# Program order for a log-decay stage, and what stands in front of the modulation dots, in a gated-linear-attention layer on one core

## The chip, the core and the metric

The kernel runs on one core of a Trainium2 chip. The core has a TensorE (PE; its weight loads are shown as PEld), a VectorE (DVE), a ScalarE (ACT), a GpSimd (POOL) and a SyncE (SP), which here issues the DMAs. Each engine works through its own queue in order and waits on semaphores. Matmuls write to PSUM banks; everything else lies in SBUF or in the chip's DRAM. The metric is the device time of one execution in microseconds (us), lower being better.

## What is computed

One layer: a token mixer (bidirectional gated linear attention in four heads beside a short convolution) and a convolutional feed-forward, over 1024 tokens of width 1024, with 256 context tokens that only give the attention its first states. Cut to what matters here:

```python
sh1, sc1, gt1, sh2, sc2, gt2 = split(silu(c) @ w_ada + b_ada, 6)        # modulation of the tokens
csh1, csc1, ... = split(silu(c_ctx) @ w_ada + b_ada, 6)                  # and of the context
hc = rmsnorm(ctx, g_pre_mix) * (1 + csc1) + csh1
pc = hc @ w_in[:, :COL_Q]                    # context keys, values, low-rank gate inputs
k, v, g_f, g_b = gla_inputs(pc)              # g = log_sigmoid(a_low @ w + b) / 16, per head and channel
s_f, s_b = gla_final_state(...)              # sum of k * exp(b_last - b) times v, b = cumsum(g)
p = (rmsnorm(x, g_pre_mix) * (1 + sc1) + sh1) @ w_in
o = gla(q, k, v, g_f, s_f) + flip(gla(flip(...), s_b))
o_gla = rmsnorm(o, g_head) * silu(og)
o_sc = sb * (w_sc[0] * left + w_sc[1] * u + w_sc[2] * right + b_sc)      # u = sc * sx, in rows of 64
x = x + gt1 * rmsnorm(concat(o_gla, o_sc) @ w_out, g_post_mix)
x = x + gt2 * rmsnorm(conv_ffn(...), g_post_ffn)
```

Products are made with about float32 accuracy: each operand is split into a rounded part `hi` and a remainder `lo` (`split`, L130: ACT copies to `hi`, DVE or POOL subtracts), and `mm3` (L142) sums three products.

## The kernel before

The program is straight-line: every loop is unrolled. TensorE runs in program order throughout. For ACT, DVE, POOL and SP a planner orders the instructions from simulated times and priorities, except inside `tc.manual_schedule(engines=...)`, where the named engines keep program order. A tile takes a buffer of its pool when its first writer is planned; that writer waits on the chip for the buffer's last reader.

**Token-major pass** (L577 to L628; ACT, DVE and POOL in program order, SP planned). 128 tokens at a time, `token_major` (L516) makes 24 matmuls of 272 columns with the tokens as the stationary operand. The first round (`g` = 2, L588, tk 0 to 7) gives the low-rank gate inputs (`als`) and 240 value columns, then context keys (`kc`, L604) and context values (`vc`, L614); the second round (`g` = 1, L618) gives the remaining 272 value columns for tokens and context. The weights of the second round are loaded by `wa_load(1, kt)` and split by `wa_split(1, kt)`: kt 0 to 3 at the end of the first round, kt 4 to 7 after the context values (L616). `ctx_norm` (L492) transposes and modulates the context two feature tiles at a time and returns the subtraction that makes their lo part (`ctx_lo`, L510). `put_aT` (L528) transposes the gate inputs of one token tile and stores them three times (hi, lo, and the raw value, which is rounded on writing).

**Modulation dots.** `w_ada` is streamed in tiles of 512 KB, 48 of them in this pass (16 for the context, 32 for the later parts of the tokens); each is multiplied with the conditioning row and summed by one DVE instruction (`ada_dot`, L231). `some_ada(n)` (L547) first does the dots of the loads that the previous call issued, then issues `n` loads into buffers lent by other pools (`few` and `many`, L544: `px`, `wraw`, `whi`, `wlo`, `ada`).

**Weight blocks.** `block(n)` (L573) streams 128 columns of `w_in` in all eight row tiles: a DMA to `raw`, `hi` on ACT at once, and `rest()`, a generator of four POOL subtractions. Block 2 is made at the end of the pass (L622), the others by `stream` (L654): `halves` (L639) multiplies a block with 512 tokens at a time, in two steps of four row tiles (12 matmuls of 512 columns each); blocks come in threes, product, second factor, third factor, of the short convolution (`sc_first`, `sc_conv`, `sc_last`).

**Log-decay stage and recurrence.** `gla()` (L723) is a generator that yields how many steps of `stream` are due; the loop at L994 interleaves the two. Its first eleven steps are the log-decay stage: two context tiles (`ctx_decay`), eight token tiles (`decay`: one gate matmul, three ACT instructions, one DVE instruction, L476), context keys' weights (`ctx_keys`, L791), cumulative sums by a triangular matrix (`sums`, L737, copied by ACT to `bc`), the context state (`ctx_state`, L804) and the first keys' weights `kx` (`kx_prep`, L753: small exponentials to `dec`, difference, exponential, product). Gate matmuls take turns in two PSUM banks (`ps_at`), and `ctx_keys`, `sums` and `ctx_state` in two others (`ps_ms`). DVE keeps program order for the first two steps only (`ORDERED = 2`); ACT is planned. Then come `kx_turn` and `update` for eight tiles, the levels of the attention, and the output.

**Output projection** (from L1229). The first two token tiles' inputs are loaded and split under a written order of ACT, DVE and SP (L1233): `so` is the convolution half, `sog` the gates, `mix_first` splits `so`, `mix_gate` applies the SiLU gate.

Of the kernel before, what the change touches and what calls it, by code (L numbers as in the profile page):

```python
# [8 lines left out]
F32 = mybir.dt.float32  # L9
# [110 lines left out]
def build(nc, ap, out, dbg=None):  # L120
# [6 lines left out]
    def act(o, i, fn=AF.Copy, **kw):  # L127
        return S.activation(o, i, fn, **kw)  # L128
# [20 lines left out]
    with tile.TileContext(nc) as tc, tc.manual_schedule(engines={mybir.EngineType.PE}):  # L149
# [378 lines left out]
        def put_aT(tk):  # L528
            pt = bank(ps_ms)
            PE.transpose(pt[:32, :P], als[tk], ident)  # L530
            s = slice(tk * P, (tk + 1) * P)
            act(aT[0:32, s], pt[:32, :P])
            V.tensor_tensor(aT[32:64, s], pt[:32, :P], aT[0:32, s].bitcast(F32), ALU.subtract)
            V.tensor_copy(aT[64:96, s], pt[:32, :P])

        def xlhs(tk):
            s = slice(tk * P, (tk + 1) * P)
# [6 lines left out]
        few = (px, "x", 8), (wp, "wraw", 2), (pgt, "ada", 1), (px, "x", 8), (wp, "wraw", 2)  # L544
        many = (px, "x", 8), (wp, "whi", 2), (pgt, "ada", 1), (wp, "wlo", 2), (px, "x", 8), (wp, "whi", 2), (wp, "wlo", 2)

        def some_ada(n, where=few):  # L547

            for a, raw in pend:
                ada_dot(a[0], a[1], raw)  # L550
            pend.clear()
            for _ in range(n):
                a = next(adas, None)
                if a is not None:
                    where_ = where[nada[0] % len(where)]
                    pend.append((a, ada_load(a[0], *where_)))
                    nada[0] += 1

        def stream_weights(src, eng):
            raw = wp.tile([P, KT, P], F32, tag="wraw", name=nm("wr"))  # L560
            SY.dma_start(raw, src)
            hi = wp.tile([P, KT, P], F32R, tag="whi", name=nm("wh"))
            lo = wp.tile([P, KT, P], F32R, tag="wlo", name=nm("wl"))
            act(hi, raw)

            def rest():
                for k in range(0, KT, 2):
                    eng.tensor_tensor(lo[:, k : k + 2], raw[:, k : k + 2], hi[:, k : k + 2].bitcast(F32), ALU.subtract)  # L568
                    yield

            return hi, lo, rest()
# [5 lines left out]
        with tc.manual_schedule(engines={mybir.EngineType.Activation, mybir.EngineType.DVE, mybir.EngineType.Pool}):  # L577
            ctx_load()
            some_ada(4)
            for hf in range(2):  # L580
                pq1 = bank(ps_mm)
                tsl = slice(hf * 512, hf * 512 + 512)
                for kt in range(KT):
                    mm3(pq1, wq1[kt], (hxh[kt][:, tsl], hxl[kt][:, tsl]), kt == 0, kt == KT - 1)
                act(qh[hf][:, 1, :], pq1, AF.Copy, scale=DK ** -0.5)
            for t in range(NT):
                vt[t] = pvo.tile([P, VW], F32, tag="vo", name=nm("v"))
            for tk in range(NT):  # L588
                some_ada((3, 3, 3, 2, 2, 1, 2, 2)[tk])
                if 4 <= tk < 8:  # L590
                    ctx_lo()
                token_major(2, tk, xlhs(tk), vt[tk])
                if tk > 1:
                    put_aT(tk - 2)
                if 3 <= tk < 7:
                    ctx_lo = ctx_norm(tk - 3)
                if tk == NT - 1:
                    for kt in range(4):
                        wa_load(1, kt)
                        wa_split(1, kt)  # L600
            put_aT(NT - 2)
            kc = px.tile([P, NCT, QK], F32, tag="x", name="kc")
            vc = px.tile([P, NCT, VW], F32, tag="x", name="vc")
            for j in range(NCT):  # L604
                pp = bank(ps_mm)
                some_ada(3)
                for kt in range(KT):
                    mm3(pp[:, :QK], hc(kt, j), (wah[0, kt][:, :QK], wal[0, kt][:, :QK]), kt == 0, kt == KT - 1)
                act(kc[:, j, :], pp[:, :QK])
            put_aT(NT - 1)  # L610
            for kt in range(4, KT):
                wa_load(1, kt)
            some_ada(3)
            for j in range(NCT):  # L614
                token_major(2, NT + j, lambda kt: hc(kt, j), vc[:, j, :])
            for kt in range(4, KT):  # L616
                wa_split(1, kt)
            for tk in range(NT):  # L618
                some_ada((3, 3, 3, 3, 3, 2, 0, 0)[tk], many)
                token_major(1, tk, xlhs(tk), vt[tk])  # L620
                if tk == NT - 2:
                    w2 = block(2)  # L622
                    for _ in w2[2]:
                        pass
                if 0 < tk <= NCT:
                    put_aT(NT + tk - 1)
            for j in range(NCT):
                token_major(1, NT + j, lambda kt: hc(kt, j), vc[:, j, :])  # L628
# [10 lines left out]
        def halves(w, nxt, dests):  # L639

            hi, lo = w[:2]
            for hf in range(2):
                bk = bank(ps_mm)
                s = slice(hf * 512, hf * 512 + 512)
                for kt in range(KT):
                    mm3(bk, (hi[:, kt, :], lo[:, kt, :]), (hxh[kt][:, s], hxl[kt][:, s]), kt == 0, kt == KT - 1)
                    if kt == KT // 2 - 1:
                        next(nxt[2], None)
                        yield
                dests(hf, bk)  # L650
                next(nxt[2], None)
                yield

        def stream():  # L654
            w = w2
            for n in range(16):
# [8 lines left out]
                    yield from halves(w, nxt, lambda hf, bk: og_out(n - 12, hf, bk))  # L665
                w = nxt

        def sc_tile(dt=F32):
            return pg_.tile([P, 512], dt, tag="sc", bufs=4, name=nm("sc"))

# [4 lines left out]
        def sc_conv(j, hf, bk, us):  # L675
            u = us[hf]
            V.tensor_tensor(u, u, bk, ALU.mult)
            y = sc_tile()
            act(y, u, AF.Identity, bias=col("bsc", j), scale=col("wsc", 3 * j + 1))
            y3, u3 = (a.rearrange("p (r c) -> p r c", c=GW) for a in (y, u))  # L680
            V.scalar_tensor_tensor(y3[:, :, 1:], u3[:, :, :-1], col("wsc", 3 * j), y3[:, :, 1:], ALU.mult, ALU.add)
            V.scalar_tensor_tensor(y3[:, :, :-1], u3[:, :, 1:], col("wsc", 3 * j + 2), y3[:, :, :-1], ALU.mult, ALU.add)
            us[hf] = y

        def sc_last(j, hf, bk, us):
            y = us[hf]
# [28 lines left out]
            split(wo_raw(0), hi, lo)  # L715
            woh[worder[0]], wol[worder[0]] = hi, lo

        ORDERED = 2
        on = [None] * NT
        pe_ = popen("pe_", "right", bufs=1)  # L720
        flat = lambda t: t.rearrange("p f t -> p (f t)")
# [1 line left out]
        def gla():  # L723
# [26 lines left out]

            kxs, kxt = {}, {}

            def kx_prep(hf, d):  # L753
                e = (P - 1) if d == 0 else 0
                for hh in range(2):
                    act(decv[d * DK : d * DK + DK, hh, :, 4 * hf : 4 * hf + 4],
                        bc[hf][d][hh * DK : hh * DK + DK].rearrange("p f (c t) -> p f c t", t=P)[:, :, :, e],
                        AF.Exp, scale=ITAU)
                kx = pe_.tile([P, 2, 512], F32, tag="e", bufs=4, name=nm("kx"))
                b3 = bc[hf][d].rearrange("p f (c t) -> p (f c) t", t=P)  # L760
                V.tensor_tensor(kx.rearrange("p f (c t) -> p (f c) t", t=P),
                                b3[:, :, e : e + 1].broadcast_to([P, 8, P]), b3, ALU.subtract)
                act(kx, kx, AF.Exp, scale=ITAU)
                V.tensor_tensor(kx, kx, kh[hf], ALU.mult)
                kxs[hf, d] = kx

            def kx_turn(c):
                pt = bank(ps_at)
# [52 lines left out]
            for c in range(NT):  # L821
                decay(c)
                if c == 2:
                    V.tensor_copy(masks, mraw)
                if 0 < c <= NCT:
                    ctx_keys(c - 1)
                if c > 1:
                    sums(c - 2)
                if c == 4:
                    su = [px.tile([P, 2, 512], F32, tag="x", name=f"su{i}") for i in range(4)]  # L830
                    ctx_state()
                if c in (5, 6):
                    kx_prep(0, c - 5)
                yield 0.8 if c > 1 else 1
            sums(NT - 2)
            yield 0.8
# [1 line left out]
            for c in range(NT):  # L838
# [6 lines left out]
                if c > 0:  # L845
                    update(c - 1)
                if c in (1, 2):
                    kx_prep(1, c - 1)
                yield 1.2
            update(NT - 1)  # L850

# [134 lines left out]
                    yield 0.8  # L986

        ga, st = gla(), stream()
        with tc.manual_schedule(engines={mybir.EngineType.DVE}):
            for _ in range(ORDERED):  # L990
                next(st)
                next(ga)
        due = 0.0
        for steps in ga:  # L994
            due += steps
            while due >= 1:
# [236 lines left out]
        with tc.manual_schedule(engines={mybir.EngineType.Activation, mybir.EngineType.DVE, mybir.EngineType.SP}):  # L1233
            so = pvo.tile([P, H, P], F32, tag="vo", name=nm("so")), t7[:, 0, :].rearrange("p (h t) -> p h t", t=P)
            dma(so[0], sc_d[0][0])
            sog = [gate_load(c) for c in range(2)]
            dma(so[1], sc_d[0][1])
            wo_raw(6)
            xts = [x1_load(c) for c in range(2)]
            wo_split(1)  # L1240
# [1 line left out]
            wo_split(2)  # L1242
            wo_split(3)
            wo_raw(7)
            mix_gate(0, sog[0])
            made.append(mix_first(so[1]))
            wo_split(4)
            split(sog[0], *(t[:, 0:4, :] for t in made[0]))
            mix_gate(1, sog[1])
# [451 lines left out]
```

## Time and profile before

| | |
|---|---|
| median of 3 runs | 1142.1 us (1141.63 to 1143.94) |
| profiled execution | 1145.11 us, its span 1143.3 us |
| granted TensorE clock, mean | 0.996 |
| idle TensorE, 0 to 75 / 75 to 150 / 150 to 197 us | 8.2 / 2.1 / 5.7 us |
| idle TensorE, 197 to 400 / 400 to 1143 us | 1.6 / 9.5 us |
| HBM read / written | 142.12 / 32.78 MB |

The idle times are the length of each stretch less the TensorE's busy time in it. A timeline row of the profile gives start, duration, engine, line, operation, output<-inputs, and in brackets the idle time before it with the instruction that ended it. L128 and L135 are the lines of helpers (`act`, the subtraction of `split`), so such rows are told apart by their tiles. A granted clock of 0.50 means that the TensorE runs at half its speed.

### The profile page before, as it was taken

How to read it: one execution, taken by the hardware profiler on the slowest of the kernel's cores; microseconds unless marked ns; L12 is line 12 of the kernel's file. 1: busy time of each engine (PE TensorE's matmuls, PEld its weight loads, DVE VectorE, ACT ScalarE, POOL GpSimd, SP SyncE). 2: the span in 40 equal slices, each digit the busy share in tenths (PEclk: the TensorE clock that was granted, in tenths of full speed). 3: DMA queues.
4: the chain of work that ended last, by engine and by line, in shares of the span. 5: the costliest groups of instructions: out<-in, count | busy, mean ns of one | idle time of the engine just before them, and what ended most of it. 6: DMA issues, size and time to landing. Idle time of an engine off the chain costs nothing. (4 is left out here: it accounts for less than half of the span.)

```text
span 1143.3 us, 16858 instructions
## 1 busy us (share of the span) xinstructions
PE 1116.2 (98%) x6256; PEld 924.3 (81%) x6256; DVE 874.5 (76%) x1193; ACT 523.6 (46%) x941; POOL 490.1 (43%) x465
## 2 busy tenths in 40 slices
PE   8999989999999999999999999999999999999997
PEld 7689977888887878887888888888888888888885
DVE  5979845699777465677799887887878788777676
ACT  6744167654343366565323333324242445544443
POOL 5200031347466111128787787777778670000002
PEclk9999999999999999999999999999999999999999
DMA  9987962312113274231244223322323269978572
GB/s 354 303 284 243 348 108 58 95 43 67 53 32 102 62 245 145 83 125 66 86 148 142 98 83 111 124 98 74 120 99 106 79 228 353 333 241 287 189 240 101
DMA packets 80132, 176.00 MB, mean 154 GB/s; under 512 B 9807, under 2 KB 21711, under 8 KB 80050
## 3 DMA queue, kind: packets, MB, share of 16 engines
q1 hardware_dynamic: 80050, 174.93, 46.1%
q8 instruction: 49, 0.80, 0.3%
q14 instruction: 33, 0.27, 0.1%
HBM read 142.12 MB, written 32.78 MB: 153 GB/s over the span
## 5 line engine op out<-in xcount | busy, mean ns | idle before, releaser
L1373 DVE SCALAR_TENSOR_TENSOR y<-u,cols,y 128x945 f32<-128x945 f32 (+2 forms) x176 | 214.8, 1222 | 3.7 <-ACT y L128 1.3
L145 PE MATMUL ps<-mx,p 128*128 128x512 f32 x440 | 173.5, 394 | 0.9 <-DVE g L1428 0.5
L146 PE MATMUL ps<-mx,p 128*128 128x512 f32 x440 | 172.5, 392 | 0.0
L147 PE MATMUL ps<-mx,p 128*128 128x512 f32 x440 | 172.5, 392 | 0.0
L135 POOL TENSOR_TENSOR p<-rs,p 128x512 fp32r<-128x512 f32 x88 | 116.6, 1329 | 86.1 <-ACT p L128 86.1
L568 POOL TENSOR_TENSOR wl<-wr,wh 128x256 fp32r<-128x256 f32 x64 | 57.9, 935 | 163.6 <-ACT wh L128 163.5
L147 PE MATMUL ps<-p,p 128*128 128x512 f32 x308 | 120.0, 390 | 0.2
L146 PE MATMUL ps<-p,p 128*128 128x512 f32 x308 | 119.9, 389 | 0.0
L145 PE MATMUL ps<-p,p 128*128 128x512 f32 x308 | 119.9, 389 | 0.0
L145 PE MATMUL ps<-hxh,wh 128*128 128x512 f32 x256 | 104.0, 406 | 1.0 <-DVE sc L687 1.0
L147 PE MATMUL ps<-hxh,wl 128*128 128x512 f32 x256 | 100.8, 394 | 0.0
L145 PEld LDWEIGHTS ps<-mx,p 128*128 128x128 f32 x440 | 82.5, 188 | 22.5 <-ACT u L128 3.2
L146 PE MATMUL ps<-hxl,wh 128*128 128x512 f32 x256 | 100.6, 393 | 0.0
L128 ACT ACTIVATE p<-rs 128x512 fp32r<-128x512 f32 x88 | 54.5, 623 | 100.6 <-POOL rs L1198 100.6
L147 PEld LDWEIGHTS ps<-mx,p 128*128 128x128 f32 x440 | 82.6, 188 | 18.7
L146 PEld LDWEIGHTS ps<-mx,p 128*128 128x128 f32 x440 | 82.6, 188 | 18.2
L135 POOL TENSOR_TENSOR p<-wr,p 128x512 fp32r<-128x512 f32 x57 | 74.0, 1298 | 10.9 <-ACT p L128 10.9
L128 ACT ACTIVATE y<-u,cols 128x1024 f32<-128x1024 f32 x22 | 26.6, 1210 | 102.9 <-DVE u L1435 102.9
L147 PE MATMUL ps<-b,p 128*128 128x512 f32 x176 | 69.5, 395 | 0.0
L145 PE MATMUL ps<-b,p 128*128 128x512 f32 x176 | 69.4, 394 | 0.0
L146 PE MATMUL ps<-b,p 128*128 128x512 f32 x176 | 69.4, 394 | 0.0
L147 PEld LDWEIGHTS ps<-p,p 128*128 128x128 f32 x308 | 57.8, 188 | 12.9 <-DVE p L135 0.8
(278 smaller groups left out, 2611.8 us busy)
## 6 DMA issues: line engine op xcount, KB each, us to landing
ada<-in_ada SPq DMA_DIRECT2D x64, 512.0 KB, 5.3
wr<-in_wu SPq DMA_DIRECT2D x48, 512.0 KB, 4.0
h<-hd SPq DMA_DIRECT2D x77, 256.0 KB, 4.3
hd<-h SPq DMA_DIRECT2D x73, 256.0 KB, 2.0
wdr<-in_wd SPq DMA_DIRECT2D x55, 256.0 KB, 3.3
wdr<-in_wd SPq DMA_DIRECT2D x22, 512.0 KB, 6.0
x<-in_x SPq DMA_DIRECT2D x16, 512.0 KB, 4.5
wr<-in_wb SPq DMA_DIRECT2D x16, 512.0 KB, 3.7
```

Source lines behind the costliest of these rows:

```text
L128: return S.activation(o, i, fn, **kw)
L135: (eng or V).tensor_tensor(lo, raw, hi.bitcast(F32), ALU.subtract)
L145: PE.matmul(ps, lh, rh, start=first, stop=False, skip_group_check=more)
L146: PE.matmul(ps, lh, rl, start=False, stop=False, skip_group_check=more)
L147: PE.matmul(ps, ll, rh, start=False, stop=last, skip_group_check=more)
L568: eng.tensor_tensor(lo[:, k : k + 2], raw[:, k : k + 2], hi[:, k : k + 2].bitcast(F32), ALU.subtract)
L1373: V.scalar_tensor_tensor(y3[:, ro, co], u3[:, ri, ci], col("wcf", 9 * p + 3 * (dr_ + 1) + dc + 1), y3[:, ro, co], ALU.mult, ALU.add)
```

## The change

- In the first round, the context's lo part and `put_aT` (its transposes too) go in front of the dots. The third store of `put_aT` is done by ACT instead of DVE.
- `some_ada` is parted: `ada_loads` only issues loads. The keys' loop asks for two loads a time instead of three, and the call before the context values issues two loads and does no dots, so the splits of the value weights (L616) follow without dots between. The second round asks for 20 loads instead of 17.
- A memset of one column of `kc` and of `vc` on POOL makes them take their buffers ahead of those loads.
- Block 2's load is issued at tk = 2 of the second round, and in every block `hi` is made in the first step of `rest()`.
- The log-decay stage's eleven steps, with the stream steps due among them, are in program order on ACT and DVE. For it `kx_prep` is parted into difference, rest, and `chunk_decay` (the small exponentials, moved behind the stage), and the taps of the first short convolution wait in `later` until the next half block.
- In the output projection, the second `so` is loaded ahead of the gates and split ahead of the first `mix_gate`.

```diff
@@ put_aT
-            V.tensor_copy(aT[64:96, s], pt[:32, :P])
+            act(aT[64:96, s], pt[:32, :P])
@@ some_ada
-        def some_ada(n, where=few):
-
-            for a, raw in pend:
-                ada_dot(a[0], a[1], raw)
-            pend.clear()
+        def ada_loads(n, where=few):
             for _ in range(n):
                 a = next(adas, None)
...
+        def some_ada(n, where=few):
+
+            for a, raw in pend:
+                ada_dot(a[0], a[1], raw)
+            pend.clear()
+            ada_loads(n, where)
+
@@ stream_weights
-            act(hi, raw)
 
             def rest():
+                act(hi, raw)
                 for k in range(0, KT, 2):
@@ token-major pass
             for tk in range(NT):
-                some_ada((3, 3, 3, 2, 2, 1, 2, 2)[tk])
                 if 4 <= tk < 8:
                     ctx_lo()
-                token_major(2, tk, xlhs(tk), vt[tk])
                 if tk > 1:
                     put_aT(tk - 2)
+                some_ada((3, 3, 3, 2, 2, 1, 2, 2)[tk])
+                token_major(2, tk, xlhs(tk), vt[tk])
...
+            G.memset(kc[:, 0, 0:1], 0.0)
+            G.memset(vc[:, 0, 0:1], 0.0)
             for j in range(NCT):
                 pp = bank(ps_mm)
-                some_ada(3)
+                some_ada(2)
...
-            some_ada(3)
+            ada_loads(2)
...
             for tk in range(NT):
-                some_ada((3, 3, 3, 3, 3, 2, 0, 0)[tk], many)
+                if tk == 2:
+                    w2 = block(2)
+                some_ada((3, 3, 3, 3, 3, 3, 2, 0)[tk], many)
                 token_major(1, tk, xlhs(tk), vt[tk])
                 if tk == NT - 2:
-                    w2 = block(2)
                     for _ in w2[2]:
                         pass
@@ halves
             for hf in range(2):
+                for f in later:
+                    f()
+                later.clear()
                 bk = bank(ps_mm)
@@ sc_conv
             V.tensor_tensor(u, u, bk, ALU.mult)
-            y = sc_tile()
...
-            us[hf] = y
+
+            def taps():
+                y = sc_tile()
...
+                us[hf] = y
+
+            if j:
+                taps()
+            else:
+                later.append(taps)
@@ gla
-            def kx_prep(hf, d):
+            def chunk_decay(hf, d):
                 e = (P - 1) if d == 0 else 0
                 for hh in range(2):
                     act(decv[d * DK : d * DK + DK, hh, :, 4 * hf : 4 * hf + 4],
...
+            def kx_diff(hf, d):
...
+            def kx_rest(hf, d):
+                act(kxs[hf, d], kxs[hf, d], AF.Exp, scale=ITAU)
+                V.tensor_tensor(kxs[hf, d], kxs[hf, d], kh[hf], ALU.mult)
...
-                if c in (5, 6):
-                    kx_prep(0, c - 5)
+                if c == 6:
+                    kx_diff(0, 1)
+                if c > 5:
+                    kx_rest(0, c - 6)
+                if c == 5:
+                    kx_diff(0, 0)
...
                 if c in (1, 2):
-                    kx_prep(1, c - 1)
+                    kx_diff(1, c - 1)
+                    kx_rest(1, c - 1)
+                if c in (1, 2, 3, 4):
+                    chunk_decay((c - 1) // 2, (c - 1) % 2)
@@ interleaving
-        with tc.manual_schedule(engines={mybir.EngineType.DVE}):
-            for _ in range(ORDERED):
+        due = 0.0
+        with tc.manual_schedule(engines={mybir.EngineType.Activation, mybir.EngineType.DVE}):
+            for _ in range(2):
                 next(st)
                 next(ga)
-        due = 0.0
+            for _ in range(ORDERED):
+                due += next(ga)
+                while due >= 1:
+                    next(st)
+                    due -= 1
@@ output projection
             dma(so[0], sc_d[0][0])
+            dma(so[1], sc_d[0][1])
             sog = [gate_load(c) for c in range(2)]
-            dma(so[1], sc_d[0][1])
...
+            made.append(mix_first(so[1]))
             mix_gate(0, sog[0])
-            made.append(mix_first(so[1]))
```

`ORDERED` is 9 after the change.

More of the change, by code (lines that the diff above doesn't have):

```diff
@@ L666, in stream @@
                 w = nxt
+        later = []
         def sc_tile(dt=F32):
@@ L677, in sc_conv @@
             V.tensor_tensor(u, u, bk, ALU.mult)
-            y = sc_tile()
[L679 to L682, printed above, removed]
-            us[hf] = y
+            def taps():
+                y = sc_tile()
+                act(y, u, AF.Identity, bias=col("bsc", j), scale=col("wsc", 3 * j + 1))
+                y3, u3 = (a.rearrange("p (r c) -> p r c", c=GW) for a in (y, u))
+                V.scalar_tensor_tensor(y3[:, :, 1:], u3[:, :, :-1], col("wsc", 3 * j), y3[:, :, 1:], ALU.mult, ALU.add)
+                V.scalar_tensor_tensor(y3[:, :, :-1], u3[:, :, 1:], col("wsc", 3 * j + 2), y3[:, :, :-1], ALU.mult, ALU.add)
+                us[hf] = y
[3 more added lines that the diff above has]
+                later.append(taps)
         def sc_last(j, hf, bk, us):
@@ L716, in wo_first @@
             woh[worder[0]], wol[worder[0]] = hi, lo
-        ORDERED = 2
+        ORDERED = 9
         on = [None] * NT
@@ L758, in kx_prep @@
                         AF.Exp, scale=ITAU)
-                kx = pe_.tile([P, 2, 512], F32, tag="e", bufs=4, name=nm("kx"))
+            def kx_diff(hf, d):
+                e = (P - 1) if d == 0 else 0
+                kxs[hf, d] = pe_.tile([P, 2, 512], F32, tag="e", bufs=4, name=nm("kx"))
                 b3 = bc[hf][d].rearrange("p f (c t) -> p (f c) t", t=P)
-                V.tensor_tensor(kx.rearrange("p f (c t) -> p (f c) t", t=P),
+                V.tensor_tensor(kxs[hf, d].rearrange("p f (c t) -> p (f c) t", t=P),
                                 b3[:, :, e : e + 1].broadcast_to([P, 8, P]), b3, ALU.subtract)
-                act(kx, kx, AF.Exp, scale=ITAU)
-                V.tensor_tensor(kx, kx, kh[hf], ALU.mult)
-                kxs[hf, d] = kx
+            def kx_rest(hf, d):
+                act(kxs[hf, d], kxs[hf, d], AF.Exp, scale=ITAU)
+                V.tensor_tensor(kxs[hf, d], kxs[hf, d], kh[hf], ALU.mult)
             def kx_turn(c):
```

## The prediction

> **What bounds the kernel now.** First the busy time on the page, then busy time by stretches, then the longest wait of the TensorE after its start.
>
> ```profile
> PE 1116.2 (98%) x6256; PEld 924.3 (81%) x6256; DVE 874.5 (76%) x1193; ACT 523.6 (46%) x941; POOL 490.1 (43%) x465
> ```
> ```profile
> 75.00:150.00 75.00, 72.87 (x563) 71.72 (x563) 63.93 (x130) 20.72 (x63) 1.71 (x3) 0.98 0.82 288
> 150.00:197.00 47.00, 41.34 (x214) 34.52 (x213) 19.47 (x27) 33.01 (x65) 11.14 (x14) 0.96 0.39 50
> 197.00:400.00 203.00, 201.40 (x1931) 167.43 (x1930) 156.09 (x229) 93.56 (x134) 97.05 (x112) 1.00 0.23 66
> ```
> ```profile
> PE ps L743 <- ACT kw L128: 2.7, 1, 2.7
> ```
>
> The second view's columns are stretch, length, busy time of PE, PEld, DVE, ACT and POOL, granted clock, DMA share, GB/s. The TensorE bounds nearly the whole span, so nothing that only makes another engine quicker can show. An edit wins where the TensorE stands still or runs at a granted clock below 1: 2.1 us and a mean clock of 0.98 in 75 to 150, 5.7 us and 0.96 in 150 to 197, but only 1.6 us in the next 203 us. The waits behind the first two figures, quoted below one by one, are all at places that the diff touches. PE's order is written by hand and unchanged but for some small transposes, so a microsecond won early passes to the end unless a later wait takes it back.
>
> **Part 1, context lo parts ahead of the dots (tk 4 to 7).**
>
> ```profile
> 105.48 0.28 PE L146 MATMUL ps<-wal,hch 128*128 128x256 f32 x1
> 106.39 0.39 PE L147 MATMUL ps<-wah,hcl 128*128 128x256 f32 x1 [0.63 <-DVE hcl L510]
> ```
> ```profile
> 101.28 0.63 ACT L128 ACTIVATE hch<-t 128x512 fp32r<-128x512 f32 x1
> ```
> ```profile
> 105.65 0.69 DVE L510 TENSOR_TENSOR hcl<-t,hch 128x512 fp32r<-128x512 f32 x1
> ```
>
> The last context lo part runs at 105.65 because two dots stand before it on DVE. Its input is ready at 101.91; in front it is done by 102.6, well before its use at 105.5. Matmuls come every 0.12 us here, so 0.91 less 0.12 is won: **0.8 us**. Queued behind the subtraction are now the dots, which can start up to 2 us later after each context tile; that is part 4's matter. The third gate-input copy (L534) goes from DVE to ACT, ten instructions of about 0.3 us; ACT is busy 20.72 of these 75 us, which hides them (uncovered: 3 us).
>
> **Part 2, value weights in front of dots.**
>
> ```profile
> 117.32 0.29 PE L147 MATMUL ps<-wah,hxl 128*128 128x272 f32 x1
> 117.93 0.39 PE L145 MATMUL ps<-wah,hxh 128*128 128x272 f32 x1 [0.32 <-ACT wah L128]
> 119.50 0.39 PE L146 MATMUL ps<-wal,hxh 128*128 128x272 f32 x1 [1.19 <-DVE wal L135]
> ```
> ```profile
> 116.84 0.37 ACT L128 ACTIVATE vc<-ps 128x240 f32<-128x240 f32 x1 [3.51 <-DVE gcol L231]
> ```
> ```profile
> 115.57 1.22 DVE L231 CUSTOM_DVE_ANT_0 ada<-ada,cb 128x1024 f32<-128x1024 f32 x1
> ```
> ```profile
> 119.01 1.49 DVE L135 TENSOR_TENSOR wal<-war,wah 128x272 fp32r<-128x272 f32 x4
> ```
> ```profile
> 120.00:123.00 3.00, 3.00 (x15) 3.00 (x15) 3.00 (x7) 0.40 (x1) 0.00 (x0) 0.50 0.99 345
> ```
>
> Two things stand ahead of the weights: on DVE three dots at a pitch of 1.15 us (115.57 to 119.01), and on ACT the copy of the context values, which waits 3.51 us for a buffer that the first of those dots holds. Matmuls come every 0.125 us, so 0.49 and 1.44 us are lost; then the clock is 0.50 for one stretch. The profile's mean of 0.98 over 75 us is 1.5 us of lost clock; the windows around it (0.96, 0.50, 0.97) give 1.7, which I take. Loss: 3.6 us.
>
> After: the memsets claim the buffers of kc and vc on POOL, which has 1.71 us of work in this whole stage; behind them in its order are only block 2's four subtractions, needed some 25 us later. No such memset is in this trace; by the shortest and longest POOL work near by (nothing, and those 1.71 us in three instructions) it costs 0 to 0.6 us each, off PE's path: 0. ACT then follows the context products. PE leaves these at about 115.1 (0.8 earlier than now); ACT empties the last bank by 115.8 and makes four hi parts, DVE four lo parts at 0.37 each, the first pair by 116.6, when PE, twelve matmuls on, asks for it. I leave 0.2 us. Won: **3.4 us**.
>
> **Part 3, log-decay in program order.**
>
> ```profile
> 149.94 0.39 PE L145 MATMUL ps<-hxh,wh 128*128 128x512 f32 x1
> ```
> ```profile
> 158.82 0.39 PE L147 MATMUL ps<-hxh,wl 128*128 128x512 f32 x1
> 159.85 0.50 PE L473 MATMUL ps<-wgh,aT 98*128 98x512 f32 x1 [0.65 <-DVE gc L482]
> 160.19 1.46 PE L798 MATMUL ps<-gc,tri 128*128 128x256 f32 x6
> 161.29 0.58 PE L145 MATMUL ps<-hxh,wh 128*128 128x512 f32 x1
> ```
> ```profile
> 165.75 1.05 PE L743 MATMUL ps<-tri,g 128*128 128x128 f32 x8
> 166.56 0.48 PE L473 MATMUL ps<-wgh,aT 98*128 98x512 f32 x1
> 169.74 1.16 PE L743 MATMUL ps<-tri,g 128*128 128x128 f32 x8 [2.70 <-ACT kw L128]
> ```
> ```profile
> 193.04 0.39 PE L147 MATMUL ps<-hxh,wl 128*128 128x512 f32 x1
> 195.74 1.13 PE L743 MATMUL ps<-tri,g 128*128 128x128 f32 x8 [2.31 <-DVE g L482]
> ```
> ```profile
> 171.00:174.00 3.00, 3.00 (x9) 2.33 (x8) 0.71 (x2) 2.01 (x5) 0.00 (x0) 0.50 0.66 179
> ```
> ```profile
> 156.34 1.08 ACT L128 ACTIVATE ge<-ps 128x512 f32<-128x512 f32 x2
> ```
> ```profile
> 160.38 0.60 ACT L128 ACTIVATE ge<-ps 128x512 f32<-128x512 f32 x1 [0.71 <-PE ps L473]
> 161.01 0.63 ACT L128 ACTIVATE ge<-ge 128x512 f32<-128x512 f32 x1
> 161.68 0.72 ACT L128 ACTIVATE ge<-ge,small 128x512 f32<-128x512 f32 x1
> 162.31 0.64 ACT L128 ACTIVATE kw<-ps 128x256 f32<-128x256 f32 x2
> 166.59 1.06 ACT L128 ACTIVATE wh<-wr 128x1024 fp32r<-128x1024 f32 x1 [3.64 <-DMA wr<-in_wb]
> ```
>
> At 0.23 us a matmul PE would have gone on at 159.05, 166.8 and 193.27: 0.8, 2.9 and 2.5 us are lost, and 1.7 in the second half clock, **7.9 us** in all. The causes: ACT works two decays interleaved (x2 at 156.34), so the first is out only with the second; ACT stands 3.64 us for the raw data of a weight block while the context keys' exponentials (L801), whose bank sums(1) needs, are queued behind; and convolution and kx work stands in front of the last g.
>
> In program order a decay alone takes ACT 1.93 us (160.38 to 162.31), then DVE about 0.7. On the clock of before: the second context decay starts at 156.34, its g is out at 159.05, and gate(1) waits 0.1 where it waited 0.8. PE then runs 0.7 ahead of now without a wait up to gate(3) (165.8) and could begin sums(1) at 166.05. ACT does decay 0 to 160.2, decay 1 to 162.15, the first keys (two of 0.32) to 162.8; the copy of block 2's second product waits for PE, to 164.1; decay 2 ends at 166.05, the second keys at 166.75. So sums(1) waits about 0.7. Behind that matmul on PE stands all else; on ACT nothing stands behind a late thing but hi of block 4 (below). Further on, sums(2) to sums(6) find inputs done 1 us and more ahead by the same count; the last g is out 1.3 us before sums(7), as the taps and the kx product no longer stand before it; the last kx product, late next, is done about when kx_turn(0) asks. Left: 0.9. Won: **7.0 us**. The eight small exponentials of chunk_decay, 0.2 us each, move to a stretch where ACT is busy 93.56 of 203 us.
>
> hi of block 4 now stands in ACT's order ahead of decay 4 and the context state. Its raw load, in this run:
>
> ```profile
> 150.53 1.06 SPq L1026 DMA_DIRECT2D row<-gv  x2
> 151.78 4.42 SPq L561 DMA_DIRECT2D wr<-in_wb  x2
> ```
> ```profile
> row<-gv SPq DMA_DIRECT2D x2, 4.0 KB, 13.7
> ```
>
> It was issued behind two row stores of 13.7 us each, hence the 166.59 above. After the change ACT asks for it at about 169.9, less the 4.2 us won by then: 165.7. Block 2 leaves its buffer some 7 us earlier, so the load can pass the stores. Between 0 and 1.5 us; I take 0, since landing then lies near the request even unhelped.
>
> **Part 4, dots that come late.** All 48 vectors still pass DVE ahead of the log-decay. DVE now waits from about 112 to 116 for the weights, with 24 dots to go: 24 x 1.15 = 27.6 us, so until 146 if the data are there.
>
> ```profile
> 110.38 30.41 SPq L221 DMA_DIRECT2D ada<-in_ada  x22
> ```
> ```profile
> 147.23 1.22 DVE L231 CUSTOM_DVE_ANT_0 ada<-ada,cb 128x1024 f32<-128x1024 f32 x1
> ```
> ```profile
> 155.22 0.69 DVE L482 SCALAR_TENSOR_TENSOR gc<-ps,ge 128x512 f32<-128x512 f32 x1 [2.12 <-ACT ge L128]
> ```
>
> But the stream is near what DMA gives: a load is issued every 1.38 us, and block 2's load goes from behind them all into their middle (tk = 2), block 3's perhaps too. The last dot, now done at 148.4, can come at 148.4, or with two blocks ahead (2.8) and 4 us of buffers freed late at 155. The first decay wants DVE at 155.2 - 4.2 = 151.0. So 0 to 4 us, with a half clock 5.7; nearest to the row of loads, which SP issues as buffers come free, I take **1.0 lost**.
>
> **Part 5, output projection.**
>
> ```profile
> 402.44 0.50 PE L145 MATMUL ps<-woh,mh 128*128 128x512 f32 x1 [0.33 <-ACT mh L128]
> ```
>
> This mh is the split of the second tile's convolution half, whose load stands behind both gate loads on SP. It goes ahead of them, and its split ahead of the first SiLU: 0.33 and a slower pitch after it, **0.5 us** won (0 if the load lands no earlier). The gate loads and the SiLU that move behind feed products four weight tiles later.
>
> **Sum:** -0.8 - 3.4 - 7.0 + 1.0 - 0.5 = -10.7 us. The profiled execution took 1145.1 us (span 1143.3), 3.0 over the median of 1142.1; the stalls lie inside the program, so I take the same off the median: **1131.4**.
>
> The half clocks stand behind idle time: 1.5 us in two waits before 119.8, 2.70 us before 171; the 2.31 us before 195.74 brought none. [...]
>
> **Rivals.**
> 1. The dots run over the start of log-decay: DMA is near its limit; against it, DVE needs only 27.6 us for the rest. -10.7 + 4 gives 1135.4. Chance 0.18.
> 2. The half clocks have another cause and stay, 3.4 us not won: 1134.8. Against it, both begin right behind a gap. Chance 0.06.
> 3. ACT in order becomes the limit (chains too long, a late raw block): it has 33.01 us of work against some 39. Half of part 3 is lost: 1134.9. Chance 0.10.
> 4. The claims don't do what they say: vc still waits for a dot, part 2 gains nothing: 1134.8. Chance 0.05.
> 5. Slower: the claims take two of the some seven buffers of the stream early (two each of px, whi and wlo, one of ada). Loads come every 1.38 x 7/5 = 1.93 us, 22 of them end 12 us later, with two blocks 14.9: dots end at 163, DVE holds the first decay 12 us, the clock halves once: 14.0 lost against 11.7 won, 1144.4. It decides from a last dot at 161. Against it: loads stand before the claims in the program. Chance 0.06.
> 6. Better: part 4 costs nothing and later waits go: 1129. Chance 0.07.
>
> The forecast, 1129.5 to 1133.3, has 0.48. **Range:** 1128 to 1138; it takes in rivals 1 to 4 with part 4's worst, and leaves out rival 5 and the tails. A measurement of this kernel tells about 0.2% (2.3 us) from no change. Faster: all but rival 5 and combinations of 1 to 4, 0.90; within 0.2%: 0.04; slower: 0.06.
>
> **What would show it.** Parts 1 and 2: no wait on hcl, wal or wah, clock 1.00 from 75 to 150. Part 3: from block 2's first matmul to sums(7) about 38.8 us in place of 45.8, no half clock, under 1 us on kw. Part 4: the last dot against the first gc. It would be wrong if PE stands for gc at the start, if ACT waits for wr with decays behind it, or if waits between 197 and 400 grow.

## The result, and the profile after

| | before | after |
|---|---|---|
| median | 1141.87 us (1141.5 to 1143.94, 4 runs) | 1136.41 us (1136.25 to 1136.97, 4 runs) |
| profiled execution, its span | 1145.11, 1143.3 us | 1136.33, 1134.5 us |
| idle TensorE, 75 to 150 / 150 to 197 / 197 to 400 us | 2.1 / 5.7 / 1.6 us | 1.8 / 0.8 / 1.6 us |

The ratio of the medians is 0.9946, with an interval of 0.9927 to 0.9966. The forecast was 1131.4 us. Between the two profiled executions 8.8 us are gone, between the medians 5.5: that difference is the first thing to explain.

Busy time on the page of after, then busy time by stretches (columns as before):

```profile
PE 1112.7 (98%) x6256; PEld 921.1 (81%) x6256; DVE 872.8 (77%) x1183; ACT 526.4 (46%) x951; POOL 494.8 (44%) x467
```
```profile
75.00:150.00 75.00, 73.22 (x572) 71.47 (x571) 59.95 (x116) 24.48 (x75) 4.08 (x5) 1.00 0.81 290
150.00:197.00 47.00, 46.19 (x250) 39.23 (x249) 28.06 (x38) 38.42 (x76) 13.67 (x14) 1.00 0.37 73
197.00:400.00 203.00, 201.45 (x1923) 167.03 (x1922) 155.07 (x230) 93.81 (x129) 96.90 (x112) 1.00 0.25 76
120.00:123.00 3.00, 3.00 (x26) 2.98 (x25) 3.00 (x5) 0.55 (x2) 0.00 (x0) 1.00 1.02 392
```

Both stretches that held the half clocks stand at 1.00. But idle time in 75 to 150 fell only from 2.1 to 1.8 us, though the waits that made it there are gone. The waits of TensorE in after (what waited, for whom; total, count, longest, in us) name what came in their place:

```profile
PE ps L147 <- POOL wl L571: 1.1, 1, 1.1
...
PE ps L145 <- ACT wh L128: 0.6, 1, 0.6
PE ps L762 <- ACT kw L128: 0.5, 1, 0.5
...
PE ps L473 <- DVE gc L482: 0.3, 1, 0.3
```

The waits on hcl, wah, wal, g and mh are no longer there, kw has fallen from 2.7 to 0.5, and weight block 2 has two waits that before did not have. The same matmuls in the timeline of after:

```profile
105.44 0.28 PE L147 MATMUL ps<-wah,hcl 128*128 128x256 f32 x1
...
146.09 0.49 PE L145 MATMUL ps<-hxh,wh 128*128 128x512 f32 x1 [0.64 <-ACT wh L128]
147.93 0.50 PE L147 MATMUL ps<-hxh,wl 128*128 128x512 f32 x1 [1.12 <-POOL wl L571]
...
154.43 0.50 PE L473 MATMUL ps<-wgh,aT 98*128 98x512 f32 x1 [0.33 <-DVE gc L482]
...
165.10 1.16 PE L762 MATMUL ps<-tri,g 128*128 128x128 f32 x8 [0.48 <-ACT kw L128]
...
187.03 1.05 PE L762 MATMUL ps<-tri,g 128*128 128x128 f32 x8
...
393.14 0.40 PE L145 MATMUL ps<-woh,mh 128*128 128x512 f32 x1
```

Since TensorE's order is the same, each matmul can be set against its counterpart in before, which gives the running difference:

| matmul | before | after | difference |
|---|---|---|---|
| context product with the late hcl | 106.39 | 105.44 | -0.95 |
| second round of the pass, behind the stall and the half clock | 123.08 | 118.50 | -4.58 |
| block 2, first product with hi | 149.94 | 146.09 | -3.85 |
| first token gate, gate(0) | 155.97 | 154.43 | -1.54 |
| sums(1) | 169.74 | 165.10 | -4.64 |
| sums(7) | 195.74 | 187.03 | -8.71 |
| output projection, mh | 402.44 | 393.14 | -9.30 |

Won, given back by 3.0 us between 118 and 154, and won again. The rows behind the part given back, on ACT, DVE, POOL and on SP's queue in after, and POOL in before:

```profile
113.94 0.36 ACT L128 ACTIVATE vc<-ps 128x240 f32<-128x240 f32 x1
...
144.97 1.06 ACT L128 ACTIVATE wh<-wr 128x1024 fp32r<-128x1024 f32 x1 [8.16 <-DVE gcol L231]
...
150.68 1.06 ACT L128 ACTIVATE wh<-wr 128x1024 fp32r<-128x1024 f32 x1 [2.49 <-DVE gcol L231]
151.65 0.58 ACT L128 ACTIVATE ge<-ps 128x512 f32<-128x512 f32 x1
```
```profile
146.07 1.23 DVE L231 CUSTOM_DVE_ANT_0 ada<-ada,cb 128x1024 f32<-128x1024 f32 x1
...
147.34 1.62 DVE L231 CUSTOM_DVE_ANT_0 ada<-ada,cb 128x1024 f32<-128x1024 f32 x1
...
148.89 1.75 DVE L231 CUSTOM_DVE_ANT_0 ada<-ada,cb 128x1024 f32<-128x1024 f32 x1
```
```profile
146.11 5.12 POOL L571 TENSOR_TENSOR wl<-wr,wh 128x256 fp32r<-128x256 f32 x3 [45.92 <-ACT wh L128]
```
```profile
148.29 2.85 POOL L568 TENSOR_TENSOR wl<-wr,wh 128x256 fp32r<-128x256 f32 x4 [89.22 <-ACT wh L128]
```
```profile
121.99 19.63 SPq L221 DMA_DIRECT2D ada<-in_ada  x15
141.68 0.43 SPq L564 DMA_DIRECT2D wr<-in_wb  x1
```

vc no longer waits, so the claimed buffers do what they say. But hi of block 2 stands still for 8.16 us on ACT. Its raw data were asked for long before (issued at 120.08); what it wants is a buffer of `whi`, and that holds a modulation vector whose dot DVE has not reached. The dots end at 150.6 where they ended at 148.4. Behind it, hi of block 3 (150.68) waits for a dot too, and the first context decay (151.65) stands behind that. Before, ACT took these two in the same order, but hi of block 3 did not wait and the decay waited only for TensorE:

```profile
151.84 1.06 ACT L128 ACTIVATE wh<-wr 128x1024 fp32r<-128x1024 f32 x1
153.17 0.60 ACT L128 ACTIVATE ge<-ps 128x512 f32<-128x512 f32 x1 [0.27 <-PE ps L473]
```

And the lo parts of block 2, which POOL used to make after the dots at 0.71 us each (2.85 for 4), are made beside the last dots, at 1.71 us each (5.12 for 3).

### The profile page after: what moved, and what is told of

The parts are those of the page before. It is cut to its first block, busy times and chain, and to the rows that moved or that the text cites. A ratio compares the mean times of both kernels' runs of the same rounds, so it can differ in the third digit from the quotient of the medians.

```text
span 1134.5 us, 16859 instructions
## 1 busy us (share of the span) xinstructions
PE 1112.7 (98%) x6256; PEld 921.1 (81%) x6256; DVE 872.8 (77%) x1183; ACT 526.4 (46%) x951; POOL 494.8 (44%) x467
## 5 line engine op out<-in xcount | busy, mean ns | idle before, releaser
L145 PE MATMUL ps<-p,p 128*128 128x512 f32 x308 | 119.8, 389 | 0.0
L571 POOL TENSOR_TENSOR wl<-wr,wh 128x256 fp32r<-128x256 f32 x64 | 62.5, 1007 | 109.1 <-ACT wh L128 94.7
```

Source lines behind the costliest of these rows:

```text
L145: PE.matmul(ps, lh, rh, start=first, stop=False, skip_group_check=more)
```

## The experiments

**Theory T.** The change's own effects are as forecast; what is given back comes from buffers of `whi` and `wlo` lent to the vectors, and from ACT's order, which puts a late hi ahead of the decays. The gap between forecast and median comes from half clocks that an execution has or has not. **Rivals:** the pass parts win little; the stage in program order gains less than it seems; ACT is simply too full. The kernel before had a median of 1142.1 us beside the first four experiments, 1142.8 beside e5 to e7, 1142.7 beside e8 to e10 and 1141.8 beside the last two.

**1. The kernel before once more.**

> The kernel before, unchanged. Theory: its profiled execution (1145.1 us) held two stretches of 3.41 us at half clock that most of its other executions do not have; each costs 1.7 us, and 1145.1 - 3.4 = 1141.7 is what the other runs show. Then this profile shows no, one or two such stretches after 15 us, and its time is about 1141.7 plus 1.7 for each. Rival: the half clocks belong to the kernel and are in every execution; then the profile shows two again, at the same two places, and the time of this run has no relation to their number.

1143.86 us (1139.85 to 1146.38, 12 runs), ratio 1.0008 (0.9997 to 1.002). The profiled execution took 1146.38 us; waits on TensorE in its timeline, then the stretches behind them:

```profile
117.83 0.39 PE L145 MATMUL ps<-wah,hxh 128*128 128x272 f32 x1 [0.31 <-ACT wah L128]
119.41 0.40 PE L146 MATMUL ps<-wal,hxh 128*128 128x272 f32 x1 [1.19 <-DVE wal L135]
...
167.56 1.16 PE L743 MATMUL ps<-tri,g 128*128 128x128 f32 x8 [0.62 <-ACT kw L128]
...
191.94 2.05 PE L743 MATMUL ps<-tri,g 128*128 128x128 f32 x8 [2.30 <-DVE g L482]
...
402.04 0.50 PE L145 MATMUL ps<-woh,mh 128*128 128x512 f32 x1 [2.21 <-ACT mh L128]
```
```profile
120.30:123.50 3.20, 3.20 (x16) 3.20 (x15) 3.20 (x6) 0.40 (x1) 0.00 (x0) 0.50 0.65 221
...
192.00:195.00 3.00, 3.00 (x13) 2.98 (x14) 0.55 (x1) 0.77 (x3) 0.00 (x0) 0.50 0.29 101
...
403.60:406.80 3.20, 3.20 (x9) 2.49 (x8) 3.20 (x5) 3.20 (x5) 0.00 (x0) 0.50 1.02 409
```

The same program has three half clocks here, two of them at other places than in the profile shown of before, where the same wait on g (2.31 us) had none. The wait on kw is 0.62 us instead of 2.70, that on mh 2.21 instead of 0.33. So half clocks, and single waits for loads, belong to an execution and not to the kernel alone.

Where the half clocks fall is not mere chance. In the traces' record of the clock they begin 31 and 46 windows of 3.413 us after the clock first became full (at 13.97 us) in before, and 32, 53 and 115 windows after it (10.95 us) in e1. So in these two executions the clock changed on a grid of 3.413 us, and the grid lay elsewhere in each. Busy time by grid windows, two of before around the wait on g, then the one of e1:

```profile
191.46:194.88 3.42, 1.97 (x9) 1.30 (x7) 3.38 (x3) 2.48 (x6) 2.21 (x2) 1.00 0.18 13
194.88:198.29 3.41, 2.55 (x17) 2.38 (x18) 1.68 (x3) 1.37 (x6) 0.00 (x0) 1.00 0.50 167
```
```profile
188.44:191.85 3.41, 1.20 (x6) 0.66 (x4) 3.32 (x4) 1.71 (x5) 1.44 (x1) 1.00 0.28 58
```

In e1 TensorE is idle for 2.21 us of one window, and the next is at half clock; in before the same wait is cut into 1.45 and 0.86 us, and none follows.

Over 84 timed executions of before (1139.5 to 1146.6 us) the mean granted clock goes with the time: 15 at 0.998 have a mean of 1141.1 us, 25 at 0.995 of 1144.5 us. Two half clocks change the mean clock by 0.003 (2 x 3.413 us at half speed of 1143) and, counted at half speed, cost 3.4 us: about that step. This is argued from the clock; only a profiled execution shows how many half clocks it has and where.

**2. The pass alone.** Before, with parts 1 and 2; block 2, the log-decay stage and the output projection as before.

```diff
+            G.memset(kc[:, 0, 0:1], 0.0)
+            G.memset(vc[:, 0, 0:1], 0.0)
...
-                some_ada(3)
+                some_ada(2)
...
-            some_ada(3)
+            ada_loads(2)
...
-                some_ada((3, 3, 3, 3, 3, 2, 0, 0)[tk], many)
+                some_ada((3, 3, 3, 3, 3, 3, 2, 0)[tk], many)
```

> Only the token-major pass is changed (context lo parts and gate inputs ahead of the dots, the third copy on ACT, memsets of kc and vc, value weights ahead of dots); block 2, the log-decay stage and the output projection are as before. Theory: 0.9 us at hcl and 1.9 us at wal and wah are won, without half clocks 2.8 us, so 1139.0; the start of the log-decay stage then shows a new wait or not, by whether block 2's hi waits for DMA or dots. Rival: the later dots take it all back at the first decays: 1141 to 1142.

1147.2 us (1145.33 to 1148.11), ratio 1.0038 (1.0024 to 1.0052): slower by 0.4%. TensorE's longest wait, and ACT's:

```profile
PE ps L145 <- ACT wh L128: 6.7, 1, 6.7
```
```profile
150.88 1.06 ACT L128 ACTIVATE wh<-wr 128x1024 fp32r<-128x1024 f32 x1 [14.17 <-DMA wr<-in_wb]
```

The theory's number missed: 4.7 us are won up to 123 us, as in after, but block 2's raw load is now issued behind all vectors (142.70 on SP's queue). TensorE waits 6.7 us, and a half clock of 10.2 us begins in that wait. What the pass wins is paid back where block 2 follows the vectors.

**3. The stage alone, and after once more.** e3 is after with the pass (parts 1 and 2) and the output projection as before: the diff of experiment 2 the other way, and put_aT, ctx_lo and so in their old places.

> Only block 2, the making of hi in the first step, and the log-decay stage in program order are changed; the pass and the output projection are as before. Theory: the three waits of the stage go except some 0.9 us, 5.3 us won without half clocks: 1136.5, since the dots here end early enough for block 2's hi. Together with the pass alone this is more than the whole change won (5.5): the difference of 2 to 3 us is what block 2's late hi costs when both are there. Rival: the stage alone also loses at its start; then 1138.5 and no such difference.

> The changed kernel again, beside the others on one chip. Theory and rival alike: 1136.4, no half clock after 15 us in its profile, waits of 0.6 us on hi and 1.1 us on lo of block 2.

e3: 1137.94 us (1136.37 to 1140.34), ratio 0.996 (0.9945 to 0.9974). e4: 1137.94 us (1134.8 to 1139.82), ratio 0.9956 (0.9941 to 0.9971). So the stage alone is worth the whole change; what the pass wins nets nothing, and sums(7) comes at 186.80 in e3 and at 187.03 in after. In e3 nothing waits for block 2. In the profiled execution of e4 the two hi parts on ACT, and TensorE's waits:

```profile
147.79 1.06 ACT L128 ACTIVATE wh<-wr 128x1024 fp32r<-128x1024 f32 x1 [9.89 <-DVE gcol L231]
...
154.13 1.06 ACT L128 ACTIVATE wh<-wr 128x1024 fp32r<-128x1024 f32 x1 [3.13 <-DVE gcol L231]
```
```profile
PE ps L145 <- ACT wh L128: 2.4, 1, 2.4
```

The same two stalls as in after, larger by 1.7 and 0.6 us, with a half clock at 150.7 besides, which was not expected.

**4. Other buffers for the last vectors.** e5: the last five vectors go to `px` and `ada`. e6: e5, with the last three dots inside the stage. e7: after, with hi and lo of block 2 made after tile 4 of the second round instead of tile 6.

```diff
e5
+        tail = {43: (pgt, "ada", 1), 44: (px, "x", 8), 45: (px, "x", 8), 46: (pgt, "ada", 1), 47: (px, "x", 8)}
...
-                    where_ = where[nada[0] % len(where)]
+                    where_ = tail.get(nada[0], where[nada[0] % len(where)])
e6, besides
-                some_ada((3, 3, 3, 3, 3, 3, 2, 0)[tk], many)
+                if tk < 6:
+                    some_ada((3, 3, 3, 3, 3, 2)[tk], many)
+                elif tk == 6:
+                    some_ada(3, many)
...
+            def late_dot():
+                if pend:
+                    a, raw = pend.pop(0)
+                    ada_dot(a[0], a[1], raw)
...
                 decay(c)
+                late_dot()
e7
-                if tk == NT - 2:
+                if tk == 4:
                     for _ in w2[2]:
```

> The changed kernel, but the last five modulation vectors are loaded into px and ada buffers only, none into whi or wlo. Theory (block 2's hi stands on ACT for a whi buffer that a vector holds until its dot): hi of block 2 is made by about 142 instead of 145 to 148, PE waits for neither hi nor lo of block 2; but three buffers carry the last five loads, so the last dot comes 1 to 4 us later and the first gate may wait for gc in its place: 1134 to 1138. Rival (block 2's hi is late because of its DMA, or ACT is late with other work): the waits on hi and lo stay as they are, 1138.

> As e5, and the last three dots are done inside the log-decay stage, one after each of the first three token tiles' decays, where DVE is idle half the time. Theory: no wait on block 2's hi or lo and none on gc at the start; 2 to 3 us better than the changed kernel, 1135 to 1136 against 1138. Rival (what is lost at the start comes from somewhere else than dots and their buffers): as the changed kernel.

> The changed kernel, but block 2's hi and lo are made after token tile 4 of the second round instead of after tile 6. Theory: hi still needs a whi buffer that a vector holds, but it gets it two tiles sooner, so PE finds hi and lo ready; the stream of vectors has two buffers fewer from there on, so the last dot comes a few us later and the wait moves to gc: 1135 to 1139. Rival as for e5: the waits on hi and lo stay.

e5: 1143.35 us, ratio 1.0006 (0.9996 to 1.0016). e6: 1143.4 us, 1.0008 (0.9997 to 1.0019). e7: 1141.47 us, 0.9985 (0.9973 to 0.9997). The waits on block 2 are gone in all three, as theory T has it; hi of block 2 in e5 no longer waits for a dot:

```profile
136.81 1.06 ACT L128 ACTIVATE wh<-wr 128x1024 fp32r<-128x1024 f32 x1
```

But all three times miss what was expected, and against before all three are slower than after. TensorE's longest wait in e5, in e6 and in e7, then hi of block 3 on ACT and its load on SP's queue in e6:

```profile
PE ps L473 <- DVE gc L482: 8.0, 1, 8.0
```
```profile
PE ps L473 <- DVE gc L482: 8.4, 1, 8.4
```
```profile
PE ps L473 <- DVE gc L482: 6.4, 1, 6.4
```
```profile
155.22 1.06 ACT L128 ACTIVATE wh<-wr 128x1024 fp32r<-128x1024 f32 x1 [8.86 <-DMA wr<-in_wb]
156.18 0.58 ACT L128 ACTIVATE ge<-ps 128x512 f32<-128x512 f32 x1
```
```profile
147.77 0.42 SPq L566 DMA_DIRECT2D wr<-in_wb  x1
```

The wait for gc names DVE, but in e6 DVE was done at 148.0 with all dots that stand ahead of the stage. What is late is the row above the decay: in program order hi of block 3 comes before it, and its raw load (147.77) is issued behind all vectors, where after issued it at 141.68. In e5 and e7 hi of block 3 waits for wr too (8.46 and 6.87 us), but there the last dots are late as well (done at 155.3 and 152.4). In these three kernels the second half of theory T, hi in front of the decays, is the larger half; experiment 5 tests it.

**5. Block 3's hi out of the decays' way.** The same three kernels with block 3's hi two stream steps later in ACT's order: e8 is e6 with it, e9 is e7, e10 is after.

```diff
                 nxt = block(3 + n) if n < 15 else (None, None, iter(()))
+                if n == 0:
+                    nxt = (*nxt[:2], itertools.chain([None] * 2, nxt[2]))
...
+                for _ in nxt[2] if n == 0 else ():
+                    pass
                 w = nxt
```

> As e6 (last five vectors in px and ada buffers, last three dots inside the log-decay stage), and block 3's hi stands two stream steps later in ACT's order, behind the first token tile's decay. Theory: in e5 to e7 the wait went from block 2's hi to block 3's, whose raw data came last from DMA and which program order puts ahead of the first decay on ACT. Then here gate(0) waits under 1 us for gc, no clock is lost, and the time is 3 us under the changed kernel's, about 1135 where that has 1138. Rival (the late gc of e6 comes from dots on DVE): the wait on gc stays near 8 us, 1143.

> As e7 (block 2's hi after tile 4), and block 3's hi two stream steps later. All dots are ahead of the stage here and end at about 152.4, where the first decay is ready for DVE at about 149.7. Theory: a wait of 2 to 3 us on gc stays, from the dots now; 1138. Rival: no better than e7, 1141.5.

> The changed kernel with block 3's hi two stream steps later and nothing else. Theory: the waits on block 2's hi and lo stay (1.7 to 2.4 us), the small one on gc goes or is the dots'; within 1 us of the changed kernel, 1137 to 1138. Rival: block 3's hi is the whole loss, 1135.

| | median | ratio to before | what still waits in its profile |
|---|---|---|---|
| e8 | 1132.98 us (1132.52 to 1133.69) | 0.9914 (0.9899 to 0.9929) | kw 0.5 |
| e9 | 1135.9 us (1134.19 to 1138.94) | 0.9941 (0.9925 to 0.9958) | gc 2.1, behind the dots |
| e10 | 1136.98 us (1135.43 to 1138.67) | 0.995 (0.9935 to 0.9965) | wh of block 2, 1.3 |

Against their twins, run on another chip where before took 1142.8 us, e8 is 10.4 and e9 5.6 us faster from that edit alone. e10 stays with after: block 2's buffer still holds it, and in the change itself the place of block 3's hi costs next to nothing. e8 and e9 are 2 us faster than was expected. ACT in e8, busy time from 75 to 150, and the matmul pair that ends with gate(0):

```profile
148.11 0.60 ACT L130 ACTIVATE ge<-ps 128x512 f32<-128x512 f32 x1 [1.34 <-PE ps L475]
...
155.11 1.04 ACT L130 ACTIVATE wh<-wr 128x1024 fp32r<-128x1024 f32 x1
```
```profile
75.00:150.00 75.00, 75.00 (x583) 73.74 (x582) 57.80 (x110) 26.66 (x78) 5.76 (x6) 1.00 0.78 270
```
```profile
150.59 0.82 PE L475 MATMUL ps<-wgh,aT 98*128 98x512 f32 x2
```

The first decay follows TensorE at 148.11, hi of block 3 comes seven microseconds later without a wait, and TensorE has no idle time left from 75 to 150. Against the profile of before, e8 is 5.1 us ahead at 119.60 (there 124.65), at block 2's first product (144.88) and at this pair (there 155.65): what after gives back is not given back here. sums(7) is 12.1 us earlier (8.7 in after).

**6. Is it the pass, or the late hi alone?** e11 is e3 (no pass parts) with block 3's hi later; e12 is e8 unchanged, on the same chip.

> e3_stage_only with block 3's hi two stream steps later, nothing else. Theory: what the pass parts win (4.6 us up to 123 us in the trace) is kept only where the handover to the log-decay stage takes nothing back; e3 has neither the pass gain nor the give-back, so moving block 3's hi finds little to win: 1136.5 to 1138, no wait on wh or gc over 0.5 us, and the waits on vc, wal and hcl in the pass stay. Rival: the late hi of block 3 alone makes the combined version fast, and the pass parts are worth nothing in it either: 1133 here too.

> e8_tail_late_hi3 unchanged, on the same chip as e11_stage_hi3 for a direct comparison. Theory: 1133, some 4 us under e11, the pass gain. Rival: both alike within 1 us.

e11: 1140.11 us (1137.56 to 1142.99, 11 runs), ratio 0.9982 (0.997 to 0.9994). e12: 1134.47 us (1133.52 to 1135.76), ratio 0.9936 (0.992 to 0.9952), 5.6 us less. e12 repeats e8 to within 1.5 us, and the rival (1133 in both) falls: without the pass parts the late hi gains nothing. e11 came out 2 us above its range; its waits on TensorE:

```profile
PE ps L147 <- ACT mh L130: 2.4, 1, 2.4
...
PE ps L148 <- DVE wal L137: 1.2, 1, 1.2
...
PE ps L149 <- DVE hcl L512: 0.6, 1, 0.6
```

wal and hcl are the waits that the pass parts remove, and a half clock stands behind wal at 119.8; the one on mh is the output projection's, whose edit e11 lacks too. e3's profile had the same wait on wal without a half clock. So the 5.6 us are the pass parts, the output projection's edit and the late dots with their buffers together. The traces part them: at 119.60 e8 is 4.6 us ahead of e11 (1.7 of it, counted at half speed, is e11's half clock), at sums(7) still 4.6, so that is the pass, kept whole; behind sums(7) comes the wait on mh.

## Why the prediction was right or wrong

- **Part 1** (0.8): 0.95 in the trace. Right.
- **Part 2** (3.4 with a half clock): 3.6 from 106 to 123 us, vc at 113.94 without a wait. Right as a mechanism. Alone it loses (experiment 2): what it wins must pass the vectors and block 2, which part 4 priced.
- **Part 3** (7.0 with a half clock): 7.2 from gate(0) to sums(7), the wait on kw 0.48 (0.7 was forecast), none for g, and hi of block 4 on ACT without idle time before it, as taken. Right, and shown apart from the pass by e3. By the prediction's own sign, from block 2's first product to sums(7), it is 40.9 us and not 38.8, as 2.3 us of part 4's loss lie in that stretch. And the size belongs to the profile it was read from: in e1's the stretch from gate(0) (155.86) to sums(7) (191.94) is 36.1 us against 39.8, since kw waited 0.62 us there and the half clock came later; against that, 3.5 us are won up to sums(7).
- **Part 4** (1.0 lost): 3.0 lost. Here a step failed. The prediction put the price on DVE, whose late dots would hold the first gc; TensorE waited 0.33 us for that. It did not follow which buffers the late dots hold: block 2's hi waits for one (0.64 us on TensorE), and its lo parts run beside the dots at 1.71 us instead of 0.71 (1.12 us). The rest is slower matmuls beside these waits (0.28 to 0.41 us from one to the next, against 0.23). e8, with other buffers, late dots and block 3's hi moved, gives none of it back. That ACT has block 3's hi ahead of the first decay was not in the sum either: in the change it cost next to nothing (e10), in e6 and e7 10.4 and 5.6 us, and there ACT waits for wr with decays behind it, which the prediction had named as a sign of being wrong. Rival 1, dots over the start of the stage, gave a time near the measured one (1135.4) for a reason that holds 0.33 us of it.
- **Part 5** (0.5): the running difference gains 0.6 from sums(7) to mh, with no wait left. Right, though not run alone; e1 and e11 show the old wait at 2.2 and 2.4 us in other executions.
- **The step to the median** failed too. "The stalls lie inside the program, so I take the same off the median": but the profiled execution of before stood 3.2 us above its median (1145.11 against 1141.87), and that of after at its median (1136.33 against 1136.41). Of the forecast 10.7 us part 4 takes 2.0, which leaves 8.7; 8.8 are gone between the profiled executions. The 3.2 us that are missing between the medians were in the profiled execution of before and not in its median. They are of the size of the two half clocks (3.4 us), and experiment 1 shows that half clocks, and the wait on kw (2.70 or 0.62 us), differ from one execution to the next. How many half clocks the median execution has, no trace shows: which of the two made the 3.2 us stays open.

So the mechanism held in parts 1, 2, 3 and 5, and the win was about half of the one forecast. The median lies in the range, but outside the forecast's own 1129.5 to 1133.3; it held since it was wide enough for part 4's worst and for rivals that did not come, and not for the step to the median, so in part by luck. Rival 2's price, 3.4 us, is the size of the step to the median, but its cause is not: the half clocks do go with the gaps, only not in every execution. Left open: the claims alone and the output projection's edit alone, which were not run, and 0.9 us that after loses again, in slower matmuls at 503 us (four with 0.33 to 0.49 us from one to the next, against 0.23) and a new wait of 0.8 us on p at 518.40.

## What to carry to other kernels

Ahead of scaling a profile to a median, take out what that one execution had by chance: list its half-clock stretches and its waits for loads, and look whether a second profile has them. The same gap can bring a half clock or not: one of 2.30 us did in e1, and one of 2.31 us, which lay across two windows of the clock's grid, did not in before. When work is moved in front of a filler stream, follow each buffer that the stream borrows to its next owner, and that owner's place in its engine's order: here, in e5 to e7, a copy for a block that is needed later stood, in program order, ahead of the decays that are needed now. The pass alone lost time, and so did other buffers alone against after; with block 3's hi moved as well they made the fastest kernel of the study (e8), so try a repair together with what it repairs.

## What the runs showed of the hardware

- The two half clocks of before lasted 3.413 us each (from 119.77 and 170.98 us), others two or three times that (6.8 us at the 6.4 us wait of e7, 10.2 us at the 6.7 us wait of e2). In a half clock the 512-column matmuls came every 0.43 us (before, 171.37 to 173.93) in place of 0.23, and the 272-column ones every 0.23 us (e1, 120.33 to 123.28) in place of 0.125. That is 1.8 to 1.9 times as long and not quite twice, so 3.41 us of it lost 1.5 to 1.6 us, where 1.7 is counted at half speed. The half clocks began whole windows of 3.413 us after the first full clock (31 and 46 in before, 32, 53 and 115 in e1). One gap of 2.3 us was followed by a half clock in e1 and by none in before, where it lay across two windows. In e1 the windows ahead of half clocks had 1.50 us of idle time in two waits (0.31 and 1.19, up to 119.41) and 2.21 us (the wait of 2.30 up to 191.94). The length of the waits alone does not decide it: in e3 two such waits (0.34 and 1.19 us, up to 119.09) brought none, and in e9 the wait of 2.1 us on gc brought none (granted clock 1.00 from 150 to 197). How those lie on the grid of their execution is not shown.
- DVE's dots and POOL's subtractions were slower where they ran at the same time. In after the dots at 147.34 and 148.89 took 1.62 and 1.75 us, those ahead of them 1.22; the three subtractions beside them took 1.71 us each (5.12 for 3), those of before, behind the dots, 0.71 (2.85 for 4). The dots read two tiles (`ada` and `cb`). About one of each got through in 1.7 us, near the sum of both durations alone (1.93). Not every dot was slowed: the one at 146.07 took 1.23 us, and a subtraction ran from 146.11 on.
